# The MLP of a decoder block as two phases of Strassen products, one up phase per chunk and one down phase for all tokens

## The chip, the cores and the metric
The kernel runs on one core of a Trainium2 chip, in one launch. The metric is the device time in microseconds. Before the change it is 2625.07 us, the median of three runs (2624.57 to 2625.38).

## What is computed
One layer of a decoder in float32: 2048 tokens of 1024 channels. A norm and an input projection feed two mixers (a gated linear recurrence and sliding-window attention); their normalised outputs go through an output projection and are added to x. Then comes the MLP, which the change is about, and a last norm:

```
x = x + jnp.einsum('bte,ed->btd', mixed, w_out[l])
hm = rmsnorm(x, norm_mlp_g[l])
up = jnp.einsum('btd,df->btf', hm, w_mlp_up[l])                                          # 1024 -> 4096
x = x + jnp.einsum('btf,fd->btd', jnp.square(jax.nn.relu(up)), w_mlp_down[l])            # 4096 -> 1024
return rmsnorm(x, norm_final_g)
```

## The kernel before
The tokens are worked on in two chunks of T = 1024. Float32 accuracy comes from splitting each operand into two float32r tiles, hi and lo: ACT copies hi, DVE subtracts to get lo (`split_weight`, L141 to 151, for weights that SP's queue loads at L144). Each product takes three matmuls: hi·hi, hi·lo, lo·hi. A matmul has a stationary tile of 128x128 and 512 moving columns.

A chunk passes through `stage1` (norm by `norm_a`, transposes on PE and splits by `norm_b`), the projections with the two mixers, the output projection (loop L673 to 719, its matmul L698, its residual added by DVE at L703), and the MLP (L722 to 788). In the last part of the output projection each of the eight token tiles of 128 tokens is normalised as it is finished, transposed and split, into tiles `hm` that stay in SBUF.

The MLP goes through 32 tiles of 128 hidden channels, two at a time. `up2` makes the two tiles for all 1024 tokens (48 matmuls each); `relu2` takes the relu and the square on ACT and splits on DVE. `down` multiplies the two by their rows of w_down for each token tile (12 matmuls for each tile, L757) and adds the result to the residual `x1[t]` in SBUF at L761. The loop at L781 puts the up of the next two tiles ahead of the down of the present two, so that PE always has matmuls whose operands are ready. Only the last `down` of a chunk normalises and stores, token tile by token tile; in the next to last one of chunk 0, `stage1` of chunk 1 is interleaved. SBUF is held by several pools with slots that follow each other (`U(i, ...)`, slots u0 to u21), and the PSUM banks are the pairs b0/b1, b2, b3 and the double banks mm0, mm1.

The scheduler places an instruction behind what it reads, within the program's order and the slots that are free; each engine then runs its own queue in order.

## Time and profile before
| what | value |
|---|---|
| median of the runs | 2625.07 us (2624.57 to 2625.38) |
| profiled execution: span | 2623.2 us |
| PE | 2577.5 us busy, 13106 instructions |
| DVE | 1474.1 us busy, 2290 instructions |
| ACT | 987.5 us busy, 1713 instructions |
| POOL | 207.4 us busy, 309 instructions |
| DMA | 159.40 MB in 45795 packets |

The span is one execution, from its first to its last recorded instruction. An engine's busy time is the time in which it worked on instructions; beside it stand the intervals in which it waited. The chain of waits follows the instruction that ended last back, step by step, to what released it. The granted clock is TensorE's clock as a share of its full 2.4 GHz.

### The profile page before, as it was taken

How to read it: one execution, taken by the hardware profiler on the slowest of the kernel's cores; microseconds unless marked ns; L12 is line 12 of the kernel's file. 1: busy time of each engine (PE TensorE's matmuls, PEld its weight loads, DVE VectorE, ACT ScalarE, POOL GpSimd, SP SyncE). 2: the span in 40 equal slices, each digit the busy share in tenths (PEclk: the TensorE clock that was granted, in tenths of full speed). 3: DMA queues.
4: the chain of work that ended last, by engine and by line, in shares of the span. 5: the costliest groups of instructions: out<-in, count | busy, mean ns of one | idle time of the engine just before them, and what ended most of it. 6: DMA issues, size and time to landing. Idle time of an engine off the chain costs nothing.

```text
span 2623.2 us, 32045 instructions
## 1 busy us (share of the span) xinstructions
PE 2577.5 (98%) x13106; PEld 2121.0 (81%) x13106; DVE 1474.1 (56%) x2290; ACT 987.5 (38%) x1713; POOL 207.4 (8%) x309
## 2 busy tenths in 40 slices
PE   7999999999999999999999999999999999999998
PEld 6887777788888888888888877778888888888887
DVE  6786658755444444444668866786544444444445
ACT  5666777214111111111446667772231212121212
POOL 1454000000000000000005530010000000000000
PEclk9999999999999999999999999999999999999999
DMA  4111114202111111111331111151021111111101
GB/s 156 41 49 49 44 43 144 92 25 78 44 56 42 57 41 56 41 57 40 112 113 41 50 50 43 43 170 63 17 89 49 49 48 49 48 49 49 48 32 65
DMA packets 45795, 159.40 MB, mean 61 GB/s; under 512 B 5328, under 2 KB 7376, under 8 KB 45648
## 3 DMA queue, kind: packets, MB, share of 16 engines
q1 hardware_dynamic: 39744, 136.12, 15.8%
q0 software_dynamic: 5760, 20.97, 2.2%
q8 instruction: 103, 1.69, 0.3%
q14 instruction: 44, 0.36, 0.0%
q10 hardware_dynamic: 144, 0.26, 0.0%
HBM read 140.56 MB, written 16.78 MB: 60 GB/s over the span
## 4 chain that ended last, share of the span: by engine, by line
PE 84%; DVE 8%; ACT 5%; issue 1%; POOL 1%; DMA 0%; SPq 0%; DVEq 0%; ACTq 0%; POOLq 0%
PE dps L757 26%; PE ops L698 12%; PE pps L194 9%; PE pps L193 9%; PE pps L196 9%; PE sc L350 2%; PE qps L193 2%; PE qps L196 2%; PE qps L194 2%; PE xps L194 1%; PE xps L193 1%; PE xps L196 1%; DVE xc L457 1%; PE av L404 1%; DVE r L630 1%
## 5 line engine op out<-in xcount | busy, mean ns | idle before, releaser
L150 DVE TENSOR_TENSOR wlo<-wraw,whi 128x1024 fp32r<-128x1024 f32 x210 | 260.1, 1243 | 431.4 <-PE pps L194 350.7
L149 ACT ACTIVATE whi<-wraw 128x1024 fp32r<-128x1024 f32 x212 | 223.1, 1056 | 684.5 <-PE dps L757 515.1
L761 DVE TENSOR_TENSOR x<-dps,x 128x512 f32<-128x512 f32 x512 | 332.9, 685 | 249.4 <-PE dps L757 249.1
L194 PE MATMUL pps<-ht,whi 128*128 128x512 f32 x1024 | 399.1, 390 | 0.0
L193 PE MATMUL pps<-ht,whi 128*128 128x512 f32 x1024 | 399.1, 390 | 0.0
L196 PE MATMUL pps<-ht,wlo 128*128 128x512 f32 x1024 | 326.3, 390 | 0.0
L757 PE MATMUL dps<-wlo,fhi 128*128 128x512 f32 x1024 | 317.1, 390 | 0.7 <-DVE wlo L150 0.5
L757 PE MATMUL dps<-whi,fhi 128*128 128x512 f32 x1024 | 316.4, 390 | 0.0
L757 PE MATMUL dps<-whi,flo 128*128 128x512 f32 x1024 | 316.1, 389 | 0.0
L698 PE MATMUL ops<-whi,ht 128*128 128x512 f32 x1024 | 282.5, 394 | 0.0
L728 ACT ACTIVATE s<-pps 128x1024 f32<-128x1024 f32 x56 | 57.5, 1027 | 493.1 <-PE pps L196 493.1
L698 PEld LDWEIGHTS ops<-whi,ht 128*128 128x128 f32 x1024 | 191.5, 188 | 44.0 <-DVE x L703 1.9
L757 PEld LDWEIGHTS dps<-wlo,fhi 128*128 128x128 f32 x1024 | 192.0, 188 | 41.7 <-DVE wlo L150 1.5
L757 PEld LDWEIGHTS dps<-whi,flo 128*128 128x128 f32 x1024 | 192.1, 188 | 40.7
L194 PEld LDWEIGHTS pps<-ht,whi 128*128 128x128 f32 x1024 | 192.3, 188 | 40.4
L196 PEld LDWEIGHTS pps<-ht,wlo 128*128 128x128 f32 x1024 | 192.3, 188 | 40.2
L193 PEld LDWEIGHTS pps<-ht,whi 128*128 128x128 f32 x1024 | 192.3, 188 | 40.1
L757 PEld LDWEIGHTS dps<-whi,fhi 128*128 128x128 f32 x1024 | 191.5, 188 | 39.7 <-ACT whi L149 0.4
L698 PE MATMUL ops<-wlo,ht 128*128 128x512 f32 x512 | 161.5, 395 | 0.0
L364 ACT ACTIVATE st<-sc,mx 128x128 f32<-128x128 f32 x256 | 91.4, 363 | 63.3 <-DVE mx L361 62.8
L698 PEld LDWEIGHTS ops<-wlo,ht 128*128 128x128 f32 x512 | 95.6, 188 | 22.0 <-DVE wlo L150 0.5
L732 DVE CAST fhi<-s 128x1024 fp32r<-128x1024 f32 x64 | 44.2, 690 | 117.2 <-ACT s L729 117.2
(200 smaller groups left out, 3854.5 us busy)
## 6 DMA issues: line engine op xcount, KB each, us to landing
wraw<-in_w_up_dram SPq DMA_DIRECT2D x64, 512.0 KB, 3.4
wraw<-in_w_down_dram SPq DMA_DIRECT2D x64, 512.0 KB, 3.4
wraw<-in_w_in_dram SPq DMA_DIRECT2D x52, 512.0 KB, 3.4
wraw<-in_w_out_dram SPq DMA_DIRECT2D x32, 512.0 KB, 3.5
xt<-in_x_dram SPq DMA_DIRECT2D x16, 512.0 KB, 4.1
ydr<-yt POOLq DMA_DIRECT2D x16, 512.0 KB, 2.9
yre<-ydr SPq DMA_DIRECT2D x16, 512.0 KB, 3.4
x<-in_x_dram POOLq DMA_DIRECT2D x16, 512.0 KB, 4.1
```

What stands on the lines that cost most here:

```text
L149: act.activation(hi, raw, AF.Copy)
L150: (eng or dve).tensor_tensor(lo, raw, f32(hi), op=ALU.subtract)
L193: pe.matmul(ps[m], w[0][:, k * P:(k + 1) * P], ht[m][0][:, k, :], start=(k == 0), stop=False)
L194: pe.matmul(ps[m], w[0][:, k * P:(k + 1) * P], ht[m][1][:, k, :], start=False, stop=False)
L196: pe.matmul(ps[m], w[1][:, k * P:(k + 1) * P], ht[m][0][:, k, :], start=False, stop=(k == KT - 1))
L350: pe.matmul(sc[:, i, :], self.q[:, b * P:(b + 1) * P], keys(self.kv, pt, b), start=(pt == 0), stop=(pt == 1))
L364: ins = act.activation(self.st[:, b, :], cur[:, i, :], AF.Exp, bias=self.mx[:, b:b + 1], accum_out=self.ls[:, b:b + 1])
L698: pe.matmul(ps[m], a_, wk[k][b_][:, hs], start=(k == 0 and a_ is yh and b_ == 0), stop=(k == kn - 1 and a_ is ylo))
L728: act.activation(s, ps, AF.Relu)
L732: dve.tensor_copy(hi, s)
L757: pe.matmul(ps[m], a_, wk[k][b_][:, hs], start=(k == 0 and a == 0 and b_ == 0), stop=(k == 1 and a == 1))
L761: dve.tensor_tensor(xs_, ps[m], xs_, op=ALU.add)
```

## The change
The up and the down product are cut into quarters, and each is made with seven products of quarters in place of eight.

Up: `Up` holds for a chunk the transposed tokens in the form of seven right operands: B11, B21, B22 and T2 are made as the output projection finishes its token tiles (`token_tile`), T4, T3 and T1 by `sums` behind it. A pair `fp` stands for two tiles of hidden channels. `weights(fp)` loads them, POOL makes sums S1, S2, S4 and A12 - A22 as float32, and ACT and DVE split all into hi and lo. `pair(fp)` runs seven products of 12 matmuls, some on top of others in one PSUM bank (S2 and S3 on A11's in pa, S4 on S1's in pr). ACT and DVE bring the results together into c1, c2, and DVE makes from their squares the seven left operands of the down products, which go to DRAM (`actd`, seven stores of 256 KB, each partition in two pieces of 1 KB). The residual x1 goes to DRAM too (`x1d`).

Down: after both chunks, PSUM becomes four tiles of two banks. `Down(g)` loads a group of four tiles of w_down and makes T1, T2, T3 and (in `split`) T4 on POOL; `act_load` brings the left operands of a block of 512 tokens back and splits them. For each g (8) and blk (4) there are seven products of 12 matmuls; after each, DVE adds its PSUM tile of 128x1024 to the residual. The next g's weights are split in block 3, one or two behind each product. `finish` normalises and stores a block in the last g.

In the output projection's last part, transposes are made for two token tiles at a time, here and in stage1 (`flip2`). All SBUF pools become one pool with fixed tags. `stage1` of chunk 1 moves into the last pair of chunk 0. Attention and the recurrence keep their work.

```diff
-    def norm_b(xn, ht, t, ps=None):
+    def norm_b(xns, ht, tp, banks):
...
+        def token_tile(self, t, src, g):
...
+            for q in range(2):
+                o12, o22 = os[q], os[2 + q]
+                t1, x3, y2 = self.braw[q][:, :, ts], self.x3[q][:, :, ts], self.y2[q][:, :, ts]
+                dve.tensor_tensor(t1, o12, t1, op=ALU.subtract)
+                act.activation(x3, o12, AF.Copy)
+                dve.tensor_tensor(y2, o22, t1, op=ALU.subtract)
+                hq = self.h["T2"]
+                act.activation(hq[0][q][:, :, ts], y2, AF.Copy)
+                dve.tensor_tensor(x3, o22, x3, op=ALU.subtract)
+                dve.tensor_tensor(hq[1][q][:, :, ts], y2, f32(hq[0][q][:, :, ts]), op=ALU.subtract)
+                hq = self.h["B22"]
+                split_ps(o22, hq[0][q][:, :, ts], hq[1][q][:, :, ts])
+        def sums(self):
...
+            for q in range(2):
+                dve.tensor_tensor(t4[q], t4[q], self.y2[q], op=ALU.subtract)
+            split("T4", ("u16", "u17", "u18", "u19"), t4)
+            split("T3", ("u6", "u3", "u5", "u4"), self.x3)
+            split("T1", ("u8", "u9", "u2", "u7"), self.braw[:2])
...
+        def weights(self, fp):
...
+            act.activation(a1h, r1, AF.Copy)
+            dve.tensor_tensor(a1l, r1, f32(a1h), op=ALU.subtract)
...
+            pool.tensor_tensor(s12[:, 0], r2[:, lo], r2[:, hi], op=ALU.add)
+            pool.tensor_tensor(s12[:, 1], s12[:, 0], r1[:, lo], op=ALU.subtract)
+            pool.tensor_tensor(r2[:, lo], r1[:, lo], r2[:, lo], op=ALU.subtract)
+            pool.tensor_tensor(r1[:, hi], r1[:, hi], s12[:, 1], op=ALU.subtract)
...
+        def pair(self, fp):
...
+            self.prod(pa, fp, "S3", "T3", False)
+            s3 = small.tile([P, HALF], F32, name="s3", tag="s3", bufs=1)
+            act.activation(s3, pa, AF.Copy)
+            c2 = self.hidden()
+            dve.tensor_tensor(c2[:, lo], pq, s3, op=ALU.add)
+            yield
+            self.prod(pr, fp, "S1", "T1", True)
+            dve.tensor_tensor(c2[:, hi], pr, s3, op=ALU.add)
...
+            self.prod(pr, fp, "S4", "B22", False)
+            dve.tensor_tensor(c1[:, hi], pr, sc[:, 1], op=ALU.add)
...
+            for o, y in enumerate((c1[:, lo], c2[:, hi], a12[:, 1], c2[:, lo], c1[:, hi], a4, a12[:, 0])):
+                nc.sync.dma_start(actd[self.c][g][:, :, o, r * 2 * P:(r + 1) * 2 * P],
+                                  y.rearrange("p (s n) -> p s n", s=2))
...
+    ps_stack.close()
+    ddp = ctx.enter_context(tc.tile_pool(name="ddp", bufs=4, space=PSUM, reuse_waits="tile"))
...
+        def split(self, name):
+            if name == "T4":
+                b21 = self.raw["B21"]
+                pool.tensor_tensor(b21, b21, self.raw["T2"], op=ALU.subtract)
+                self.raw["T4"] = b21
+            self.w[name] = split_to(BW[name], self.raw[name], name)
...
+    PRODS = (("A11", "B11", 0, (0,)), ("A22", "T4", 1, (2,)), ("S2", "T2", 0, (1,)),
+             ("A12", "B21", 2, (0,)), ("S3", "T3", 0, (2,)), ("S4", "B22", 1, (1,)),
+             ("S1", "T1", 0, (3,)))
+    SPLITS = (("B11",), (), ("T2",), ("B21", "T4"), ("T3",), ("B22",), ("T1",))
...
+        pool.tensor_tensor(four[1], four[1], four[2], op=ALU.add)
+        pool.tensor_tensor(four[1], four[1], four[3], op=ALU.subtract)
...
+    def finish(blk):
...
+        dve.tensor_tensor(a12, a12, a22, op=ALU.add)
+        dve.tensor_tensor(a12, a12, a21, op=ALU.subtract)
+        for i in range(2):
+            for h_, (l_, r_) in enumerate(((a11, a12), (a21, a22))):
+                ss = [sumsq(y[:, i, :], "fin") for y in (l_, r_)]
+                act.activation(ss[0], ss[1], AF.Identity, bias=ss[0])
+                rs = rstd_of(ss[0], 1, "fin")
...
+    for g in range(NG):
+        nxt = None
+        for blk in range(NB):
...
+                for d_ in dst:
+                    dve.tensor_tensor(accs[blk][d_], o, accs[blk][d_], op=ALU.add)
+                if last and nxt:
+                    for nm in SPLITS[n]:
+                        nxt.split(nm)
+                if n == 1 and blk == 1 and g + 1 < NG:
+                    nxt = Down(g + 1)
+                if n == 2 and (g + 1 < NG or not last):
+                    gn, bn_ = divmod(g * NB + blk + 1, NB)
+                    nops = act_load(gn, bn_)
```

How it moves instructions, at two places. The first is on PE in the middle of the up work. Before, its rows are the up product of one tile, pps from whi and wlo:

```order
L196 MATMUL pps_6291<-ht_5463,wlo_6288 128x512
L193 MATMUL pps_6291<-ht_5461,whi_6287 128x512
L194 MATMUL pps_6291<-ht_5462,whi_6287 128x512
L193 MATMUL pps_6291<-ht_5463,whi_6287 128x512
L194 MATMUL pps_6291<-ht_5464,whi_6287 128x512
L196 MATMUL pps_6291<-ht_5461,wlo_6288 128x512
L196 MATMUL pps_6291<-ht_5463,wlo_6288 128x512
```

After the change, the last four rows of the next pair's product on pb come between S1's and S4's products on qr; hm_5487 and its like are parts of B21 and B22, s4 is the split of S4:

```order
L385 MATMUL qr_6952<-hm_6001,s12l_6856 128x512
L385 MATMUL pb_7090<-hm_5489,a1h_6985 128x512
L385 MATMUL pb_7090<-hm_5487,a1l_6986 128x512
L385 MATMUL pb_7090<-hm_5487,a1h_6985 128x512
L385 MATMUL pb_7090<-hm_5489,a1h_6985 128x512
L385 MATMUL qr_6952<-hm_5819,s4_6863 128x512 [waits DVE_49]
L385 MATMUL qr_6952<-hm_5821,s4_6863 128x512
```

The matmuls on qr that add S4 now wait for DVE, which no row of the up product did before; the 12 matmuls of S1 end just ahead of the first row shown.

The second place is DVE in the down work. Before, around a turn from one pair of hidden tiles to the next, with wlo the split of a weight and x1 the residual:

```order
L150 TENSOR_TENSOR wlo_8198<-wraw_8195,whi_8197 128x1024 [waits DMAHW6_49,Activation_49]
L761 TENSOR_TENSOR x1_4601<-dps_8055,x1_4601 128x512 [waits PE_49]
L761 TENSOR_TENSOR x1_4601<-dps_8056,x1_4601 128x512 [waits PE_49]
L150 TENSOR_TENSOR wlo_8204<-wraw_8201,whi_8203 128x1024 [waits DMAHW7_49,Activation_49]
L150 TENSOR_TENSOR wlo_8338<-wraw_8335,whi_8337 128x1024 [waits DMAHW0_49,PE_49]
L732 CAST fhi_8129<-s_8126 128x1024 [waits Activation_49]
L733 TENSOR_TENSOR flo_8130<-s_8126,fhi_8129 128x1024 [waits DVE_49]
L150 TENSOR_TENSOR wlo_8400<-wraw_8397,whi_8399 128x1024 [waits DMAHW1_49,PE_49]
L761 TENSOR_TENSOR x1_4587<-dps_8207,x1_4587 128x512 [waits PE_49]
```

After the change, at the end of a g's block 3 and the start of the next g's block 0; T3l, T4l, B22l, T1l are weight splits, al and as1 splits of left operands, acc the residuals:

```order
L949 TENSOR_TENSOR T3l_16763<-braw_16437,T3h_16762 128x1024 [waits Activation_49]
L949 TENSOR_TENSOR T4l_16746<-braw_16439,T4h_16745 128x1024 [waits Activation_49]
L949 TENSOR_TENSOR al_16718<-araw_16715,ah_16717 128x1024 [waits DMAHW5_49,PE_49,Activation_49]
L1061 TENSOR_TENSOR acc_16280<-dd_16672,acc_16280 128x1024 [waits DVE_49]
L992 TENSOR_TENSOR as1_16723<-araw_16721,as1_16723 128x512 [waits DMAHW6_49,Activation_49]
L949 TENSOR_TENSOR B22l_16780<-braw_16441,B22h_16779 128x1024
L1061 TENSOR_TENSOR acc_16284<-dd_16654,acc_16284 128x1024
L949 TENSOR_TENSOR T1l_16797<-t1_16443,T1h_16796 128x1024 [waits Activation_49]
L1061 TENSOR_TENSOR acc_16183<-dd_16800,acc_16183 128x1024 [waits PE_49]
L1061 TENSOR_TENSOR acc_16187<-dd_16814,acc_16187 128x1024 [waits PE_49]
L949 TENSOR_TENSOR al_16844<-araw_16841,ah_16843 128x1024 [waits DMAHW0_49,Activation_49]
L1061 TENSOR_TENSOR acc_16185<-dd_16800,acc_16185 128x1024 [waits PE_49]
```

The accumulations that read dd from PSUM stand in one queue with the seven weight splits of the next g, where before two weight splits and two splits of hidden tiles stood between 16 additions.

## Rows read from the trace of the kernel before
**Rows 1.** The page's busy time, share of the span and instructions of each engine.
```profile
PE 2577.5 (98%) x13106; PEld 2121.0 (81%) x13106; DVE 1474.1 (56%) x2290; ACT 987.5 (38%) x1713; POOL 207.4 (8%) x309
```

**Rows 2.** Busy us of each engine by stretch, with granted clock, DMA share, GB/s.
```profile
0.00:25.00 25.00, 13.37 (x57) 10.69 (x58) 18.96 (x35) 19.16 (x38) 6.79 (x11) 1.00 0.85 322
...
618.00:663.00 45.00, 45.00 (x205) 36.97 (x204) 16.96 (x20) 15.79 (x23) 0.00 (x0) 1.00 0.34 116
663.00:1275.00 612.00, 612.00 (x2700) 506.22 (x2700) 264.91 (x343) 116.92 (x126) 0.00 (x0) 1.00 0.15 48
...
2570.00:2624.00 54.00, 45.39 (x199) 36.75 (x197) 35.24 (x54) 16.42 (x32) 0.00 (x0) 0.96 0.20 78
```

**Rows 3.** The chain of waits, chunk 0's MLP: start us, us, what.
```profile
615.80 1.93 PE tps L184 x16
...
663.66 21.80 PE dps L757 x96
...
707.23 21.80 PE dps L757 x96
```

**Rows 4.** Groups by line and shape: busy us, mean ns, then idle before.
```profile
L761 DVE TENSOR_TENSOR x<-dps,x 128x512 f32<-128x512 f32 x512 | 332.9, 685 | 249.4 <-PE dps L757 249.1
...
L150 DVE TENSOR_TENSOR wlo<-wraw,whi 128x1024 fp32r<-128x1024 f32 x210 | 260.1, 1243 | 431.4 <-PE pps L194 350.7 <-ACT whi L149 51.3 <-PE kps L194 11.5
L149 ACT ACTIVATE whi<-wraw 128x1024 fp32r<-128x1024 f32 x212 | 223.1, 1056 | 684.5 <-PE dps L757 515.1 <-PE ops L698 141.5 <-DMA wraw<-in_w_out_dram 22.0
...
L733 DVE TENSOR_TENSOR flo<-s,fhi 128x1024 fp32r<-128x1024 f32 x64 | 78.2, 1221 | 1.2
...
L703 DVE SCALAR_TENSOR_TENSOR x<-ops,rs_lr,x 128x512 f32<-128x512 f32 x64 | 45.2, 746 | 60.2 <-PE ops L698 60.2
...
L174 DVE SCALAR_TENSOR_TENSOR xn<-x,rs_mlp,g 128x1024 f32<-128x1024 f32 x16 | 20.5, 1284 | 0.5
...
L457 DVE SCALAR_TENSOR_TENSOR xc<-xps,vec,xc 128x1022 f32<-128x1022 f32 x16 | 20.4, 1276 | 0.0
...
L431 DVE TENSOR_TENSOR acca<-acca,yq 128x512 f32<-128x512 f32 x28 | 18.6, 701 | 7.0 <-ACT yq L428 7.0
...
L639 POOL TENSOR_TENSOR accq<-accq,r 128x1024 f32<-128x1024 f32 x2 | 4.7, 2362 | 3.3 <-ACT r L638 3.3
```

**Rows 5.** The timeline, chunk 1's last down: start us, us, engine, line.
```profile
2604.43 0.62 PE L757 MATMUL dps<-whi,flo 128*128 128x512 f32 x2
...
2604.86 0.69 DVE L761 TENSOR_TENSOR x<-dps,x 128x512 f32<-128x512 f32 x1 [0.18 <-PE dps L757]
```

**Rows 6.** The timeline of POOL beside chunk 0's output projection.
```profile
457.76 2.36 POOL L639 TENSOR_TENSOR accq<-accq,r 128x1024 f32<-128x1024 f32 x1 [1.66 <-ACT r L638]
```

**Rows 7.** The timeline of DVE in the same stretch.
```profile
457.82 3.51 DVE L646 SCALAR_TENSOR_TENSOR ht<-yre,vec,ht 128x512 fp32r<-128x512 f32 x2
```

**Rows 8.** The timeline at the end of the kernel.
```profile
2615.54 0.39 PE L757 MATMUL dps<-whi,flo 128*128 128x512 f32 x1
...
2616.20 0.63 ACT L163 ACTIVATE junk<-x 128x512 bf16<-128x512 f32 x1 [0.31 <-DVE x L761]
2616.73 0.19 ACT L163 ACTIVATION_READ_ACCUMULATOR junk<-x 128x1 f32 x1
...
2618.03 0.29 ACT L156 ACTIVATE rs_fin<-ss_fin,epst 128x1 f32<-128x1 f32 x1
2618.36 0.16 DVE L157 RECIPROCAL rs_fin<-rs_fin 128x1 f32<-128x1 f32 x1 [0.35 <-ACT rs_fin L156]
...
2620.00 0.37 ACTq L771 DMA_DIRECT2D out_dram<-x  x1
```

**Rows 9.** What PE waited for: us in total, times, longest us.
```profile
PE tps L184 <- DVE prevm L127: 7.8, 1, 7.8
```

**Rows 10.** The page's DMA queues: packets, MB, share of 16 engines' time.
```profile
q1 hardware_dynamic: 39744, 136.12, 15.8%
```

More of the change, by code (lines that the diff above doesn't have):

```diff
@@ L166, in new_h, with hk @@
     def new_h():
-        return [[hpool.tile([P, KT, HALF], F32R, name="ht", tag="ht") for _ in range(2)]
-                for _ in range(2)]
+        return [[[H(n, part, kp, "ht") for kp in range(KT // 2)] for part in range(2)]
+                for n in range(2)]
+    def hk(parts, k):
+        return parts[k // 2][:, k % 2, :]
     def norm_a(src, xn, g, nm):
@@ L238, in steps @@
                 g = load(t, g)
[L239 to L242 removed]
+            for tp in range(NT // 2):
+                for t in (2 * tp + 2, 2 * tp + 3):
+                    if t < NT:
+                        load(t, g)
+                if c == 0 and tp % 2:
+                    ps = pair(0, "tps") + pair(1, "tps")
+                else:
+                    ps = mm_halves("tps", 0) + (mm_halves("tps", 1) if c == 0 else pair(0, "tps"))
+                norm_b([xs.pop(2 * tp), xs.pop(2 * tp + 1)], ht, tp, ps)
@@ L779, in hybrid_block_kernel @@
-        steps = None
-        prev = up2(0)
-        for f0 in range(0, NF, 2):
-            cur = prev
-            if f0 + 2 < NF:
-                prev = up2(f0 + 2)
-            if f0 + 4 == NF and c + 1 < NCH:
-                hn, steps = stage1(c + 1)
-            down(f0, cur, steps, f0 + 2 == NF)
-            steps = None
+                        nc.sync.dma_start(x1d[c][t * P:(t + 1) * P, :], x1[t])
+                        if t == 2:
+                            up.weights(0)
+                        up.token_tile(t, x1[t], g2)
@@ new lines, in hybrid_block_kernel @@
+    for g in range(NG):
+        nxt = None
+        for blk in range(NB):
+            ps = {}
+            last = blk + 1 == NB
+            for n, (an, bn, bi, dst) in enumerate(PRODS):
+                first = bi not in ps
+                if first:
+                    ps[bi] = ddp.tile([P, 2, HALF], F32, name="dd", tag="dd")
+                o = ps[bi]
+                ah, al = ops[an]
+                bh, bl = dn.w[bn]
+                for i in range(2):
+                    for r in range(2):
+                        t0 = r * 2 * P + i * P
+                        for k, (a_, b_) in enumerate(((ah, bh), (ah, bl), (al, bh))):
+                            pe.matmul(o[:, i, :], a_[:, t0:t0 + P], b_[:, r, :],
+                                      start=first and r == 0 and k == 0, stop=r == 1 and k == 2,
+                                      skip_group_check=True)
+                for d_ in dst:
[8 more added lines that the diff above has]
+                    nops = act_load(gn, bn_)
+            ops = nops
+            if g + 1 == NG:
+                finish(blk)
+        dn = nxt
```

369 lines of the change are left out of this document (258 added, 111 removed).

## The prediction
> **What bounds the kernel now.** I read the page's busy shares first: PE is busy for 2577.5 us, 98% of the span of 2623.2, and no other engine passes 56% [rows 1]. Then the stretches [rows 2]: from 663 to 1275 us, the middle of chunk 0's MLP, PE is busy 612.00 of 612.00 us, DVE 264.91, POOL not at all, DMA at 0.15 of its capacity. Nothing but matmuls sets the time there, and the hand-over from the output projection to the MLP (618 to 663) is just as full. The chain of waits gives the price of one matmul: a group of 96 on dps takes 21.80 us, and groups start 43.57 us apart (663.66, 707.23) with 96 up and 96 down matmuls in between [rows 3], so 43.57/192 = 0.2269 us each. The sum below is made against the profiled execution (span 2623.2); the median of the three runs, 2625.1, lies 1.9 above it, and I add that at the end.
>
> **What goes.** Before, a chunk's MLP has 1536 up and 1536 down matmuls of 128x512, 6144 in all. Seven products of 12 make an up pair or a down block, 84; there are 32 of each, 5376. So 768 matmuls go, at 0.2269: **−174.3 us**. This holds only where PE stays full, so the rest is a list of places where it no longer does.
>
> **Up phase.** A pair is 84 × 0.2269 = 19.06 us of PE. Per pair DVE has three splits of 1024 (1.24 each), one of 512, four PSUM adds of 0.69 and four sums of 0.70 [rows 4]: 10.0 us. ACT is near that. POOL has four sums of 512 elements; POOL's 1024 takes 2.36 [rows 4], so half of it, about 1.2 each. All fit under 19. The one tight hand-over is S1 to S4: both go into bank pr, and DVE must read S1 (L418) before S4 is added on top of it. Four matmuls of the next pair lie in between (the order rows ahead). In the trace a matmul that started at 2604.43 let DVE start at 2604.86 [rows 5]; 0.43 + 0.69 + 0.04 = 1.16 us against 5 × 0.2269 = 1.13. That costs 0.03 us a pair; I take **+2** for all 32, from 0 to 30 (0.9 a pair, if nothing covered it).
>
> **Output projection to up, twice.** Each of the last four token tiles now asks DVE for two residuals (0.75), a norm (0.16 + 1.28) and half of ten 512-element operations (0.69): 6.4 us, where PE has 24 matmuls, 5.45. After the last matmul DVE still owes: residual, norm and transposes until about 6.3, then ten operations of 0.69, two sums of 1.22, six splits of 1.24, c1 and a1l, 18.7 more. That is 25.0, with the backlog of four tiles 28.8. PE owns 16 transposes (1.93 for 16 [rows 3]) and 66 matmuls before it needs a1l, 16.9 us. So 11.9, with some waits in the tiles before 13 each: **+26** (8 to 18 each). This was free before (45.00 of 45.00).
>
> **Up to chunk 1's projections.** stage1(1) moves into one pair, and some of its tiles take the place of B22, which the pair's last product reads; norm splits and transposes of a quarter of the chunk follow it. At 1.06 + 1.24 a split: **+8** (3 to 15).
>
> **Up to down.** POOL's T2 and T4 sums (2.36 each) start after the last pair's c1 sum frees a slot (0.43 + 0.69), ACT's split adds 1.06: T4 is ready at 6.9 us, while PE has one product of 2.7 us without it. That is 4.2; the last S1-S4 hop, now bare, 1.2; the third accumulation behind two more POOL sums, 3.5; block 1's splits queued behind the seventh accumulation, 3. **+12** (6 to 22).
>
> **Down.** DVE's accumulation of 128x1024 from PSUM is not in the trace. Nearest lies L457, 128x1022 from PSUM at 1.276; below it L733, 1024 from SBUF at 1.221, above it two adds of 0.685, 1.37 [rows 4]; I take 1.25, nearest to L457, which also has one input in PSUM. Blocks 0 to 2 of a g: 7 × 1.25 + 3 × 1.24 + 0.70 = 13.2 us against 19.06, free. Block 3 carries the seven weight splits of the next g as well, 8.7 more: 21.9 against 19.06, and in DVE's order (ahead) the seventh accumulation stands behind six of them. The four PSUM tiles let PE run ahead, but the next block's second tile waits for the seventh accumulation's place in the queue. There is a second cost. When POOL ran a 1024 sum from 457.76 to 460.12 [rows 6], two DVE operations with both inputs in SBUF took 3.51 us [rows 7] where 512 elements take 0.75 each (L703's form, [rows 4]): one of them stood until POOL was done. The T4 sum runs in block 3, and T3's split would stand so. Laid out by hand, the seventh accumulation ends at about 25.2 us of a block in which PE wants its tile at 21.8: 3.4 us, seven times, **+24** (1 to 6 each: 7 to 42).
>
> The Trainium skill, page "SBUF — State Buffer", section "Who interferes with whom", says the same of the two engines: a VectorE operation with two SBUF inputs and a GpSimd operation that reads SBUF take one shared port pair in turn, whole instruction by whole instruction, and one that reads PSUM does not. This speaks against a change that adds some 170 POOL sums; the trace agrees (3.51 us in place of 1.5). By that rule the sum is as it stands; without it the +24 would be about +9, since 2.2 of each 3.4 us is that wait.
>
> **Last g, tail, start.** finish() puts 9.1 us of DVE into each of the last blocks, 22.3 against 19.06 where two follow each other: **+6** (2 to 10). Before, the last output's DMA is issued at 2620.00, 4.5 us after the last matmul's start at 2615.54 [rows 8]. After, it needs 0.43, the accumulation 1.25, two sums of 1.22, then on ACT seven sums of squares (0.63 + 0.19), eight of 0.29 and three DMA issues of 0.37, together 9.2, then 0.16 + 2 × 0.75 on DVE: 15.0. **+10** (8 to 13). Transposing by twos at the start: **+1** (−1 to 4).
>
> **Sum.** −174 + 2 + 26 + 8 + 12 + 24 + 6 + 10 + 1 = −85, a span of 2538, and with the 1.9 us **2540**. All costs at their low ends are 41 (time 2492), at their high ends 172 (time 2623).
>
> **Rivals.**
> (a) *The hand-overs hide.* PE's order shows it can take later products early, and the trace's waits of PE in all of the kernel before are small, 7.8 us the longest [rows 9]. If only the tail, a part of the start of up and 1 us per g are paid, 35 us: 2625 − 174 + 35 = 2486. Against it: DVE's sums for T3, T4 and T1 are plain work with nothing beside it. 12%.
> (b) *DVE sets the pace of down.* If the accumulation costs 1.37 and the weight splits shift further, 6 us at each of seven turns and 2 us more in each of the other 24 blocks: +18 + 48, 2606. For it: the queue is in order and block 3 is over-full; against it: blocks 0 to 2 have 6 us of room. 8%.
> (c) *Slower than before: the stores of up.* Each pair writes seven arrays of 256 KB in pieces of 1 KB, 1792 packets, beside 1 MB of loads. Queue q1 used 15.8% of 16 engines for 39744 packets [rows 10], 0.167 us for one of 3.4 KB. If a 1 KB packet takes as long, a pair needs (1792 + 256) × 0.167/16 = 21.4 us of DMA, more than PE's 19.06; if it takes time by its bytes, 8.8. The buffers a12, a4 and hidden are rewritten each pair, so a DMA bound becomes PE's. It decides against the change where a pair takes 85/32 = 2.7 us more than 19.06, from 0.17 us a packet with nothing lost to gaps. At 24 us a pair, 0.19 us a packet, the time is 2540 + 32 × 4.9 = 2697. Against it: the first 25 us moved 322 GB/s [rows 2], a pair wants 151. 6%.
> (d) *The clock falls after the new gaps.* The granted clock is 1.00 in all stretches with PE full, and also in the first 25 us, where PE worked 13.37 of 25.00 and once waited 7.8; only the last stretch has 0.96 [rows 2, 9]. If the 62 us of new gaps in the forecast were each followed by as long at 1.2 GHz instead of 2.4, 31 us are lost: 2571. 4%. The Trainium skill, page "TensorE: Matmul & The Clock Gate", Part 1, has the clock fall after idling; the first 25 us here do not show it.
> That it does not drop the matmuls is no rival: the order of PE's rows has 84 to a pair and a block.
>
> **How the numbers follow.** The forecast (costs of 41 to 172 us, most likely 60 to 130) has 70%, (a) 12, (b) 8, (c) 6, (d) 4. The range starts at (a)'s 2486, which lies just below the forecast's low end; above it leaves out (c), the half of (b) that passes 2600 and the forecast's last 23 us, together some 15%: **2486 to 2600**. A measurement of this kernel tells apart about 0.2%, 5 us. Faster: all but (c)'s upper half, the forecast's extreme end and a reserve for a stall I have not seen: 0.90; same 0.03; slower 0.07.
>
> **What would show it.** In the profile after: 84 matmuls per 19.1 us in up and in blocks 0 to 2 of down, PE full there; gaps of PE of some 12 us before up's T products, twice; gaps near 3 us at seven turns from block 3 to block 0, ended by DVE's L1061; T3's split near 3.5 us while POOL runs L973; the last matmul some 18 us ahead of the span's end. Wrong if up pairs take over 20 us (S1-S4 or the stores), if the turns have no gap or one in every block, or if matmuls run at 0.44 us after a gap.

## The result and the profile after

The changed kernel takes **2559.45 us** (median of four runs, 2556.74 to 2562.31) against 2624.97 for the kernel before on the same chip: ratio 0.975, 95% interval [0.9736, 0.9764]. The forecast was 2540 in a range of 2486 to 2600. The profiled execution took 2559.54 us, its span is 2557.8: 65.4 less than before's 2623.2, where the sum said 85.

The page of the kernel after: busy times, then the DMA queue of [rows 10].

```profile
PE 2436.4 (95%) x12338; PEld 1983.8 (78%) x12338; DVE 1764.7 (69%) x2377; ACT 1237.1 (48%) x2066; POOL 500.5 (20%) x469
...
q1 hardware_dynamic: 127984, 256.47, 29.7%
```

Against [rows 1], PE has 13106 − 12338 = 768 matmuls fewer, as forecast, but its share of the span fell from 98 to 95%. DVE gained 291 us and POOL 293.

Stretches of the kernel after, in the form of [rows 2]: the middle of an up phase, the down phase behind its first block, and the hand-over between them.

```profile
700.00:900.00 200.00, 200.00 (x867) 160.71 (x866) 110.40 (x125) 99.29 (x116) 62.16 (x43) 1.00 0.43 147
1970.00:2470.00 500.00, 493.59 (x2169) 405.86 (x2168) 394.56 (x333) 147.31 (x153) 64.90 (x25) 1.00 0.38 120
1860.00:1965.00 105.00, 84.45 (x330) 66.18 (x329) 69.58 (x58) 32.50 (x37) 41.85 (x16) 0.90 0.68 230
```

The up phase is full. The down phase lacks 6.4 us in 500. The 105 us around the hand-over lack 20.6, at a mean clock of 0.90. What PE waited for there (us in total, times, longest us):

```profile
PE dd L1057 <- ACT T4h L948: 6.9, 1, 6.9
PE qr L385 <- DVE hid L415: 6.0, 1, 6.0
PE dd L1057 <- DVE acc L1061: 4.4, 3, 3.1
...
```

The 6.9 of the row on T4h only looks like the forecast's "T4 is ready at 6.9 us": the wait forecast there was 4.2, behind one product of PE. In the trace T4's first matmul starts at 1912.67, 10.3 us after the last up matmul (1902.38). The row on L415 is one the forecast did not have: in the last pair of up, S1 must wait until DVE has read A22's half of the same tile.

**Where the time went.** PE's stretches between the starts of the same matmuls in both traces (us):

| stretch | before | after | lost |
|---|---|---|---|
| first matmul to first v transposes | 47.98 | 52.98 | 5.0 |
| to the output projection, both chunks | 747.62 | 747.95 | 0.3 |
| output projection, chunk 0; chunk 1 | 185.83; 185.83 | 192.46; 189.18 | 6.6; 3.4 |
| its end to chunk 1's v transposes | 738.04 | 375.05 | 29.1 over its matmuls |
| chunk 1's last output projection to the last matmul | 702.4 | 974.6 | 54.4 over its matmuls |
| last matmul's start to the end | 7.63 | 18.11 | 10.5 |

The two rows "over its matmuls" leave out what the moved and dropped matmuls take at 0.2269 us: 1728 fewer in the first (392.1), 960 more in the second (217.8). Together 109 us are lost, against 89 in the forecast: −174.3 + 109 = −65.3.

**The clock.** After the change, the granted clock falls to one half, 1.2 GHz in place of 2.4, in nine stretches ahead of the last, each within or behind waits of PE; the records of the kernel before have a fall in the last stretch alone [rows 2]. Two of them with their columns as in [rows 2], and the sums over all nine:

```profile
585.50:592.30 6.80, 5.07 (x13) 4.09 (x14) 4.44 (x5) 1.44 (x3) 0.59 (x1) 0.50 0.19 77
640.00:647.00 7.00, 6.45 (x15) 4.20 (x14) 7.00 (x8) 7.00 (x9) 4.26 (x3) 0.51 0.16 63
...
sum 54.70, PE 43.15 PEld 32.68 DVE 41.04 ACT 28.68 POOL 14.87; mean PE 4.79 PEld 3.63 DVE 4.56 ACT 3.19 POOL 1.65
```

The price, from PE's timeline inside the sixth stretch and just behind the seventh (start us, us, operation): matmuls start 0.43 apart (1893.38, 1893.81), afterwards 0.23 (1903.60, 1903.83).

```profile
1893.38 0.63 PE L385 MATMUL qr<-hm,s12h 128*128 128x512 f32 x1
1893.81 0.63 PE L385 MATMUL qr<-hm,s12l 128*128 128x512 f32 x1
...
1903.60 0.39 PE L1057 MATMUL dd<-B11h,ah 128*128 128x512 f32 x1
1903.83 0.40 PE L1057 MATMUL dd<-B11l,ah 128*128 128x512 f32 x1
```

Some 80 matmuls of 512 columns start in the nine stretches; at 0.2 us each about 16 us are lost there, an estimate from these rows (PE's 43 busy us, halved, bound it at 21.6). It is a price, not a measured cost: where other waits would take its place the clock cost less, and in experiment 6 they did. The costs exceed the forecast by 20 us; how much of that is the clock is not shown.

The 1.00 that [rows 2] gives for the first 25 us of the kernel before is not a measured clock. Its trace has no record of the clock ahead of 22.0 us, and the view counts such time as full. PE's timeline of that kernel shows the lower level there: 128x128 transposes start 0.21 us apart at 13 us, and 0.11 apart at 23 us.

```profile
13.02 1.97 PE L184 MATMUL tps<-ident,xt 128*128 128x128 f32 x8 [0.75 <-DVE ht L188]
...
23.32 0.60 PE L184 MATMUL tps<-ident,xt 128*128 128x128 f32 x4
```

So the kernel before ran at half clock too, from its first matmuls, behind a wait of 7.8 us, to about 22 us.

**DVE beside POOL.** DVE's timeline at the hand-over, then POOL's, in the kernel after:

```profile
1883.04 1.22 DVE L949 TENSOR_TENSOR B11l<-braw,B11h 128x1024 fp32r<-128x1024 f32 x1
1884.17 3.40 DVE L949 TENSOR_TENSOR al<-araw,ah 128x1024 fp32r<-128x1024 f32 x1
1887.50 3.35 DVE L949 TENSOR_TENSOR B22l<-braw,B22h 128x1024 fp32r<-128x1024 f32 x1
1890.78 0.68 DVE L415 TENSOR_TENSOR hid<-qr,s 128x512 f32<-128x512 f32 x1
...
1906.51 2.82 DVE L428 TENSOR_TENSOR a<-hid 128x512 f32<-128x512 f32 x1
...
1942.86 2.34 DVE L1061 TENSOR_TENSOR acc<-dd,acc 128x1024 f32<-128x1024 f32 x2
```

```profile
1883.62 2.87 POOL L965 TENSOR_TENSOR t<-braw 128x1024 f32<-128x1024 f32 x1 [21.54 <-DMA act<-hid]
1886.57 3.20 POOL L967 TENSOR_TENSOR braw<-braw 128x1024 f32<-128x1024 f32 x1
...
1903.09 2.41 POOL L1015 TENSOR_TENSOR acc<-acc 128x1024 f32<-128x1024 f32 x1
1905.46 3.32 POOL L966 TENSOR_TENSOR t<-braw,t 128x1024 f32<-128x1024 f32 x1
1908.86 2.67 POOL L973 TENSOR_TENSOR braw<-braw,t 128x1024 f32<-128x1024 f32 x1
...
1942.36 2.81 POOL L967 TENSOR_TENSOR braw<-braw 128x1024 f32<-128x1024 f32 x1
```

A split of 1.22 us takes 3.40 when a POOL sum starts during the operation ahead of it: it ends 1.1 us after that sum (1883.62 + 2.87 = 1886.49). A sum of 0.69 takes 2.82. An operation with an input in PSUM does not stand: two accumulations take 2.34 us from 1942.86, inside POOL's L967, and of the 294 additions and subtractions on DVE that read PSUM and start while POOL works, none takes over 1.23. L415 is of that kind, but POOL stood still at 1890.78; it came late because it stands in the queue behind two lengthened splits, and PE waits 6.0 us for it. POOL's own sums take up to 3.32 where an undisturbed one takes 2.37. T4's delay has POOL's queue in it as well: two residual sums (the last is L1015) stand ahead of T2's and T4's sums, L966 and L973, until 1905.5.

### The profile page after: what moved, and what is told of

It reads as the page before. It is cut to its first block, busy times and chain, and to the rows that moved or that the text cites. A ratio compares the mean times of both kernels' runs of the same rounds, so it can differ in the third digit from the quotient of the medians.

```text
span 2557.8 us, 32559 instructions
## 1 busy us (share of the span) xinstructions
PE 2436.4 (95%) x12338; PEld 1983.8 (78%) x12338; DVE 1764.7 (69%) x2377; ACT 1237.1 (48%) x2066; POOL 500.5 (20%) x469
## 3 DMA queue, kind: packets, MB, share of 16 engines
q1 hardware_dynamic: 127984, 256.47, 29.7%
q10 hardware_dynamic: 576, 1.05, 0.1%
## 4 chain that ended last, share of the span: by engine, by line
PE 61%; DVE 15%; issue 12%; ACT 8%; DMA 2%; POOL 2%; POOLq 0%; DVEq 0%; SPq 0%; ACTq 0%
PE ops L916 10%; PE qr L385 10%; PE dd L1057 9%; PE pa L385 9%; PE pb L385 3%; PE sc L568 2%; PE qps L226 2%; PE qps L223 2%; PE qps L224 2%; DVE xc L675 2%; DVE acc L1061 1%; PE xps L224 1%; PE xps L223 1%; PE xps L226 1%; PE av L622 1%
## 5 line engine op out<-in xcount | busy, mean ns | idle before, releaser
L1061 DVE TENSOR_TENSOR acc<-dd,acc 128x1024 f32<-128x1024 f32 x224 | 272.4, 1221 | 130.0 <-PE dd L1057 122.2
L948 ACT ACTIVATE ah<-araw 128x1024 fp32r<-128x1024 f32 x96 | 101.9, 1062 | 327.6 <-PE dd L1057 306.4
L166 ACT ACTIVATE whi<-wraw 128x1024 fp32r<-128x1024 f32 x84 | 88.5, 1055 | 119.6 <-PE ops L916 87.0
L167 DVE TENSOR_TENSOR wlo<-wraw,whi 128x1024 fp32r<-128x1024 f32 x82 | 104.5, 1279 | 38.7 <-PE kps L224 12.0
L949 DVE TENSOR_TENSOR al<-araw,ah 128x1024 fp32r<-128x1024 f32 x96 | 129.4, 1351 | 0.5 <-ACT ah L948 0.5
L223 PE MATMUL qps<-ht,whi 128*128 128x512 f32 x256 | 108.3, 423 | 0.0
L224 PE MATMUL qps<-ht,whi 128*128 128x512 f32 x256 | 101.9, 398 | 0.0
L223 PE MATMUL xps<-ht,whi 128*128 128x512 f32 x256 | 101.5, 396 | 0.0
L226 PE MATMUL qps<-ht,wlo 128*128 128x512 f32 x256 | 101.1, 395 | 0.0
L224 PE MATMUL xps<-ht,whi 128*128 128x512 f32 x256 | 100.9, 394 | 0.0
L223 PE MATMUL gpps<-ht,whi 128*128 128x512 f32 x256 | 100.8, 394 | 0.0
L385 PE MATMUL qr<-hm,s 128*128 128x512 f32 x384 | 98.6, 406 | 1.8 <-DVE hid L418 1.8
L224 PE MATMUL gpps<-ht,whi 128*128 128x512 f32 x256 | 100.1, 391 | 0.0
L973 POOL TENSOR_TENSOR braw<-braw,t 128x1024 f32<-128x1024 f32 x8 | 19.5, 2432 | 396.9 <-issue 396.8
```

The source lines that it names most:

```text
L166: act.activation(hi, raw, AF.Copy)
L167: (eng or dve).tensor_tensor(lo, raw, f32(hi), op=ALU.subtract)
L223: pe.matmul(ps[m], w[0][:, k * P:(k + 1) * P], hk(ht[m][0], k), start=(k == 0), stop=False)
L224: pe.matmul(ps[m], w[0][:, k * P:(k + 1) * P], hk(ht[m][1], k), start=False, stop=False)
L226: pe.matmul(ps[m], w[1][:, k * P:(k + 1) * P], hk(ht[m][0], k), start=False, stop=(k == KT - 1))
L385: pe.matmul(ps, w[a_][:, ks], hk(h[b_], k), start=first and k == 0 and i == 0, stop=k == KT // 2 - 1 and i == 2, skip_group_check=True)
```

## The experiments

Beside each experiment stand runs of the kernel before, and its ratio is to those.

**1. All of the change's sums on DVE instead of POOL.** 168 sums move: four per pair, four per group of down, eight for the blocks' first residuals.

```diff
-    pool = nc.gpsimd
+    pool = nc.vector
```

> All MLP sums that POOL makes (four of 512 per up pair, four of 1024 per down group, eight for the residuals) move to DVE, nothing else. Theory L (POOL's sums are the price of the hand-overs: DVE operations with two SBUF inputs stand while POOL works, 3.40 and 3.35 us in place of 1.22 around 1885 us, and the norm's square root queues on ACT behind a split that waits for POOL): the 30 us lost between 1870 and 1960 us fall to about 15, the 3.8 us wait at 583 us goes, time 2535 to 2545. Theory Q (the hand-overs are the amount of DVE's own work in its queue, so more work there makes them longer): 16 sums of 1.22 us join the queue at the last hand-over and 0.7 x 4 each up pair, time 2565 to 2575. Both: the seven turns in down stay near 1.1 us, since T3's split loses 1.35 us of standing and T4's sum costs 1.22.

Measured: 2523.52 us (2522.05 to 2523.76), ratio 0.9612 [0.9598, 0.9627], **36 us less** than the change, although DVE has more to do. That is theory L's direction, beyond its 2535 to 2545; and no wait is left at the seven turns, where both theories kept 1.1 us. DVE's timeline there at the same hand-over, and PE's waits in the 105 us around it:

```profile
1874.24 0.69 DVE L415 TENSOR_TENSOR hid<-qr,s 128x512 f32<-128x512 f32 x1
1874.84 1.22 DVE L949 TENSOR_TENSOR B22l<-braw,B22h 128x1024 fp32r<-128x1024 f32 x1
```

```profile
PE dd L1057 <- ACT T4h L948: 4.3, 1, 4.3
PE dd L1057 <- DVE acc L1061: 2.6, 2, 1.6
PE qr L385 <- DVE hid L415: 2.4, 1, 2.4
...
```

All splits are back at 1.22 and the waits, small ones included, fall from 20.6 to 10.1 us. By stretches the gain is 5.0 and 1.7 in the output projections, 2.3 and 10.3 in the ups, 16.5 in down. The half-clock stretches shrink as well, from nine to five (37.5 us in place of 54.7).

**2. One product twice.** The fourth product of every group and block of down is computed twice, and the second result overwrites the first; DVE adds it once. That is 32 × 12 = 384 matmuls more.

```diff
+                for rep_ in range(2 if n == 3 else 1):
+                    for i in range(2):
...
```

> Each down block makes its fourth product (A12 with B21) twice, the first thrown away: 12 x 32 = 384 more matmuls, no more work elsewhere. If PE bounds down: + 384 x 0.2269 = + 87.1 us less at most 7.5 us of turns that the longer block may hide, so 2639 to 2647. If DVE or the transfers bound down: under + 40, below 2600.

Measured: 2643.68 us (2641.93 to 2646.85), ratio 1.0071 [1.0054, 1.0088]: **+84.2**, where 384 × 0.2269 = 87.1. So PE does bound the down phase, a matmul there costs nearly its full price, and the −174 of the sum is priced rightly.

**3. A11's and A12's weights earlier.** For pair 1 of up they are loaded and split ahead of the sums for T4, T3 and T1 (`weights_a`, a part of `weights`), the rest behind.

```diff
...
+            part = self.weights_a(1)
...
-                if i == 1:
-                    self.weights(1)
...
+            self.sums()
+            self.weights(1, part)
```

> The load and hi/lo split of the second pair's A11, A12 are written ahead of the sums T4, T3, T1, so that PE has 24 matmuls (5.4 us) more before it needs them. Theory Q (PE waits there for DVE's queue, 25 to 29 us of work after the last output projection): each of the two gaps shrinks by about 4 us, and the half-clock stretch at 640 and 1579 us (2.6 us each by the matmuls that start in it) shrinks or goes: 2546 to 2553. Rival (PE waits for T4's and T3's splits themselves, later now by 1.2 us): 2558 to 2562.

Measured: 2560.33 us (2557.0 to 2563.61), ratio 0.9754 [0.9739, 0.9768]: no gain, as the rival had it. DVE works without a pause from 636 to 661 us there, so what is taken ahead of one operation stands behind another: the last split of the stretch ends at 660.7, in the change at 657.3. That agrees with DVE's total as the bound there; it does not show it alone.

**4. T4's product later.** In the first block of down it moves from second to fifth place.

```diff
+    LATE = tuple(PRODS[i] for i in (0, 3, 2, 4, 1, 5, 6))
...
-            for n, (an, bn, bi, dst) in enumerate(PRODS):
+            for n, (an, bn, bi, dst) in enumerate(PRODS if g or blk else LATE):
```

> In the very first down block alone the product that needs no sum of weights, A12 with B21, comes second, and T4's and T2's come after it. Theory C (PE waits 6.9 us for T4 because POOL makes it last): 2.7 us of work moves into that wait: 3 to 6 us less, 2553 to 2557. Rival (the next wait takes over: the residual's sums on POOL at 1920 us hold the accumulations and with them PSUM): under 2 us less.

Measured: 2564.47 us (2560.12 to 2567.0), ratio 0.9768 [0.9753, 0.9782]: no gain, if anything a loss. PE's waits at the hand-over, of this kernel:

```profile
PE dd L1058 <- DVE acc L1062: 7.7, 3, 3.7
PE qr L385 <- DVE hid L415: 6.0, 1, 6.0
PE dd L1058 <- ACT T4h L948: 4.2, 1, 4.2
```

T4h's wait falls from 6.9 to 4.2, the accumulations' rises from 4.4 to 7.7: one wait took the place of the other.

**5. POOL busy beside the kernel of experiment 1.** Eight POOL sums of 512 elements that nobody reads, per group of down; DVE still makes all the real ones. If POOL's share of the memory is the cause, these must cost time; if only the late sums were, they are free.

```diff
+            for k in range(8):
+                z = small.tile([P, HALF], F32, name="s3", tag="s3", bufs=1)
+                nc.gpsimd.tensor_tensor(z, b11[:, k % 2], b22[:, k % 2], op=ALU.add)
```

> The kernel no_pool (2523.5 us) and beside it POOL sums that nobody reads: for each group of down weights eight of 512 elements, about 10 us, as soon as two of its weights have landed. Theory L (what costs is that DVE operations with two SBUF inputs stand still while POOL works): in the hand-over to down, DVE's splits and sums of 1.22 us become 2 to 3.5 us where POOL runs beside them, the sum of its first product comes later, and 3 to 8 us are lost there; in the middle of down, where DVE has room, next to nothing: 2526 to 2532. Rival (what cost was that POOL's results came late; standing beside it is harmless): 2522 to 2525.

Measured: 2531.85 us (2528.74 to 2533.94), ratio 0.9645 [0.9631, 0.9659], **8.3 us more** than experiment 1. POOL's timeline in this kernel, then DVE's:

```profile
1879.53 16.16 POOL L970 TENSOR_TENSOR s<-braw 128x512 f32<-128x512 f32 x8 [479.33 <-DVE hid L418]
```

```profile
1886.71 2.28 DVE L966 TENSOR_TENSOR t<-braw,t 128x1024 f32<-128x1024 f32 x1
1888.92 1.75 DVE L428 TENSOR_TENSOR a<-hid 128x512 f32<-128x512 f32 x1
```

L966 takes 2.28 us instead of 1.22 and L428 1.75 instead of 0.68, beside sums whose result goes nowhere, and PE's wait for T4h at this hand-over grows from 4.3 to 8.8. That is the wait itself, apart from any dependency.

**6. PE kept busy at the starts of up.** 24 matmuls whose result is overwritten, ahead of pair 1 in both chunks (two further times A12's product).

```diff
+            if fp == 1:
+                for _ in range(2):
+                    self.prod(pb, 0, "A12", "B21", True)
```

> The changed kernel with 24 matmuls whose result is thrown away, written where PE waits for DVE at the start of each up phase (just before the second pair's products). Theory K (after the gaps there TensorE runs at half its clock for a while, which costs 2.6 us at each place): the granted clock at 640 and at 1579 us stays 1.00, the 5.4 us of thrown-away work lies in the waits, 2553 to 2558. Rival (the clock's fall comes from elsewhere, or the thrown-away work delays the transposes): the clock still falls, 2559 to 2566.

Measured: 2560.27 us (2557.48 to 2562.01), ratio 0.9753 [0.9739, 0.9768]: no gain. The same stretch as above (640) in this kernel, and the one at chunk 1's start of up:

```profile
640.00:647.00 7.00, 5.53 (x21) 3.17 (x19) 7.00 (x8) 6.80 (x9) 3.42 (x2) 1.00 0.17 68
1579.00:1585.00 6.00, 4.35 (x11) 2.90 (x11) 6.00 (x5) 5.01 (x7) 5.15 (x3) 0.73 0.00 0
```

The half clock at 640 is gone, and at 1579 partly: the clock did as theory K had it, the time as its rival. In each chunk 24 × 0.2269 = 5.4 us of matmuls came on top and cost nothing, so PE had been waiting there anyway, and a clock that falls in such a place costs little.

**7. A shorter tail.** Squares are summed as each quarter is done, and the two halves are normalised together.

```diff
+        for k in (0, 2, 3):
+            squares(k)
...
+        squares(1)
+        for h_, (l_, r_) in ((1, (a21, a22)), (0, (a11, a12))):
```

> Only the last norm of a block is written differently: squares summed per tile as each is final (a11, a21, a22, then a12), four roots in two instructions, the second half's rows scaled first. Forecast's step (the chain of ACT and DVE behind the last matmul, 15.0 us, sets the end): about 10.5 us of it remain, the end comes 13 to 14 us after the last matmul in place of 18.0: 2554 to 2556. Rival (the eight output transfers set the end): 2558 to 2561.

Measured: 2559.24 us (2555.93 to 2561.98), ratio 0.975 [0.9735, 0.9764]. In the profile the tail itself shrank from 18.11 to 15.16 us, but the whole did not move. The time is the rival's; its reason, the output transfers, is not shown. The last matmul starts at 2539.74 in the change and 2544.27 here, the last issue of a store at 2554.56 and 2554.75: 3 us less in the tail and 4.5 more ahead of it, where the four runs of either kernel spread by 6.

**8. No POOL sums, no POOL splits at the start, and the tail of 7.**

```diff
-    pool = nc.gpsimd
+    pool = nc.vector
...
-            wkv = [split_weight(w_in[KT * 3 + i], eng=nc.gpsimd) for i in range(2)]
+            wkv = [split_weight(w_in[KT * 3 + i]) for i in range(2)]
```

> no_pool with the tail's edit, and the two key/value weight splits at the kernel's start on DVE in place of POOL. no_pool was 2523.5; the tail gives 4 to 5; at the start a 128x8 operation of 0.17 us stood 2.26 us beside POOL's split and held the transposes behind it, 1 to 4: 2514 to 2519. Rival (the two splits, 2.4 us more in DVE's queue there, give it back): 2518 to 2521.

Measured: 2522.59 us (2519.23 to 2526.74), ratio 0.9616 [0.96, 0.9632]. It lies above both expectations; beside experiment 1's 2523.52 it is no difference that these runs can tell.

**9. POOL's sums replaced at the hand-over alone** (first group of down and the residuals' quarters), POOL elsewhere.

```diff
+            pool = nc.gpsimd if g else dve
+            self.pool = pool
...
-                pool.tensor_tensor(b21, b21, self.raw["T2"], op=ALU.subtract)
+                self.pool.tensor_tensor(b21, b21, self.raw["T2"], op=ALU.subtract)
...
-        pool.tensor_tensor(four[1], four[1], four[2], op=ALU.add)
-        pool.tensor_tensor(four[1], four[1], four[3], op=ALU.subtract)
+        dve.tensor_tensor(four[1], four[1], four[2], op=ALU.add)
+        dve.tensor_tensor(four[1], four[1], four[3], op=ALU.subtract)
```

> Only the sums at the last hand-over move from POOL to DVE: the first group's four and the residuals' eight. no_pool took 36 us off in all. If the last hand-over holds what POOL's sums cost: down's first blocks lose 14 to 16 us less, nothing else moves, 2543 to 2549. If the loss there is the order of the queues and no_pool's gain lies in up and at the turns: under 6 us, 2554 to 2559.

Measured: 2552.64 us (2547.23 to 2554.79), ratio 0.9722 [0.9708, 0.9737]: 6.8 less than the change, between the two expectations. L415's wait falls from 6.0 to 2.5 and T4h's from 6.9 to 4.4, but the accumulations' rises to 6.1. POOL's timeline there shows what stands beside them:

```profile
1932.50 3.25 POOL L968 TENSOR_TENSOR t<-braw,t 128x1024 f32<-128x1024 f32 x1
```

Free of the first group's sums, POOL makes the next group's from 1929.9 to 1938.5 (one of the three is shown), beside the first blocks of down, where DVE is still behind.

**10. T4's sum on DVE at the seven turns alone**, POOL elsewhere.

```diff
+            self.pool = dve if g else nc.gpsimd
...
-                pool.tensor_tensor(b21, b21, self.raw["T2"], op=ALU.subtract)
+                self.pool.tensor_tensor(b21, b21, self.raw["T2"], op=ALU.subtract)
```

> Only T4's sum of the groups after the first moves from POOL to DVE, seven operations. The forecast had 3.4 us at each of seven turns, measured were 1.08, and no_pool had none, where I had expected 1.1 to stay. If the wait of T3's split beside POOL (2.57 in place of 1.22 us) is all of a turn: no wait at the seven turns, 7 us less, 2551 to 2554. If the turns went because T1's to T3's sums left POOL too: 1 us stays at each, 2558 to 2561.

Measured: 2552.58 us (2550.26 to 2557.07), ratio 0.9727 [0.9713, 0.9742]: 6.9 less. In the change PE's only waits of that kind between 1965 and 2480 us were these, in this kernel there is none:

```profile
PE dd L1057 <- DVE acc L1061: 6.4, 7, 0.9
```

Seven waits of 0.9 us, one in each block 0 behind a turn, and gone with seven POOL sums: the mechanism of the forecast at a quarter of its size.

**11. Gaps put into the kernel before**, to see the clock without the change: 24 copies of a weight tile onto itself on ACT, at four places of chunk 0's MLP.

```diff
+            if c == 0 and f0 in (8, 14, 20, 26):
+                for _ in range(24):
+                    act.activation(wk[1][0], f32(wk[1][0]), AF.Copy)
```

> The kernel before, in which TensorE's clock is 1.00 throughout, with 24 copies of a weight onto itself put in a row on ACT at four places of chunk 0's MLP, so that PE stands there for some 8 to 15 us. Theory K (a wait of PE is followed by a stretch at half clock): the time grows by PE's waits and 2.5 to 3.4 us more at each of the four places, and the granted clock shows four stretches of 0.5. Rival (the clock falls for another reason than waits): the time grows by the waits alone, clock 1.00.

Measured: 2627.16 us (2626.55 to 2627.63), ratio 1.0009 [0.9999, 1.0019]. The experiment failed: no gap arose. From 900 to 1000 us, where one of the bursts lies, PE was busy 99.72 us, at clock 1.00. It says nothing of the clock. It shows that ACT had room there: four bursts of 24 copies of 1.05 us, some 100 us of work, cost 2.5 us (2626.55 to 2627.63 against 2624.06 to 2625.61).

**12. Experiment 8 with the order of 4.** The diffs are those two together.

> best1 with t4_late's order of products in the first down block. There PE waits 4.3 us for T4's split, and the residuals' sums, now on DVE, are done early, so that the wait that took over in t4_late (accumulations behind POOL's sums) is gone: the way from the last up product through the first two blocks gets 2 to 4 us shorter, 2518 to 2521. Rival: DVE's queue (sums, splits) is what PE waits for there, whatever the order: 2521 to 2524.

Measured: 2525.02 us (2524.74 to 2527.17), ratio 0.9622 [0.9608, 0.9636]: above both expectations; the order gains nothing without POOL's sums either. The fastest kernels remain those of experiments 1 and 8, some 2523 us, 1.4% below the change and 3.9% below the kernel before.

## Why the prediction was right, and where its steps were off

The direction, the size and the range held: the costs came to 109 us, inside the stated 41 to 172. The agreement is partly luck, errors that cancel, so each term is set against its measure. The turns and the last g were too large by 21 us together, and the hand-overs, S1 to S4 and the start too small by some 40.

| term | forecast | measured, in part estimated |
|---|---|---|
| 768 matmuls | −174.3 | −174.3, priced |
| S1 to S4, 32 pairs | 2 | about 10.5 |
| output projection to up, both | 26 | about 28 |
| stage1(1), up to chunk 1 | 8 | about 15 |
| up to down | 12 | about 30 |
| seven turns | 24 | about 8 |
| last g | 6 | about 1 |
| tail | 10 | 10.5 |
| start | 1 | 5.0 |

Start and tail are stretches of the table above. The others divide its long stretches by counting matmuls at 0.2269 us, and where one term ends and the next begins can shift 2 to 6 us between neighbours: the hand-over to up comes to 34 when all of 627.02 to 716.64 and 1565.12 to 1656.00 is given to it.

**The signs that were named.** From the second g on, blocks take 19.04 us, a little over 20 in block 0 behind each of the seven turns, where a gap is ended by L1061; and the last matmul starts 18.1 us ahead of the end. So far it is as told. The gaps of some 12 us ahead of up's T products are not there: the waits come in pieces, the longest 2.1 us. And one of the signs of being wrong came true: matmuls 0.43 us apart behind gaps. The sum had no term for the clock. Rival (d) had it, and set against it the first 25 us of the kernel before; against what (d) says of them, they show half clock behind a wait, and so speak for it.

**The matmuls** are right: experiment 2 prices 384 of them at 84.2 us where 87.1 was due.

**Up, S1 to S4: too small.** A pair takes 19.40 us in place of 19.06. PE's timeline in the kernel after, one pair's first S1 to the next one's:

```profile
716.64 0.73 PE L385 MATMUL qr<-hm,s12h 128*128 128x512 f32 x2
...
736.04 0.74 PE L385 MATMUL qr<-hm,s12h 128*128 128x512 f32 x2
```

The step counted one hand-over of 0.03; there are two, since S1 also waits for L415 to read the other half of the same tile. PE's matmuls start late at these two places alone, and together they cost 0.34 a pair, inside the term's 0 to 30. It is not POOL's doing: without its sums a pair still takes 19.38.

**Output projection to up: right in size**, 26 against about 28, **but not by the wait it named.** The step let PE wait for a1l at the end of DVE's debt. In experiment 3 a1l's split starts at 645.45 in place of 654.91 and nothing is gained; PE's waits in the change are mostly for the hm splits (L331, L343). That the debt as a whole sets the time is argued. Something was left out as well: at 583 us the square root of a norm stood in ACT's queue behind a split that waited for POOL's sum, and PE waited 3.8 us for the norm (1.1 in experiment 1, where no split waits for POOL). POOL's timeline, then ACT's:

```profile
581.33 1.29 POOL L363 TENSOR_TENSOR s<-s,wraw 128x512 f32<-128x512 f32 x1
```

```profile
582.66 1.06 ACT L367 ACTIVATE s12h<-s 128x1024 fp32r<-128x1024 f32 x1 [3.16 <-POOL s L363]
583.62 0.28 ACT L173 ACTIVATE rs_mlp<-ss_mlp,epst 128x1 f32<-128x1 f32 x1
```

**Up to chunk 1: inside 3 to 15.** The largest single wait, 5.5 us, is one that the step did not name: PE's for the split of a weight tile of chunk 1's first projection (kps, L223). SP issues that load at 963.73, behind two stores of the last pair and two loads of stage1. No run moved that load; in experiment 1 the wait is 5.5 us as well.

**Up to down: mis-sized, 12 against 30**, above its 6 to 22. This is the step that failed most. It had a wait of 4.2 us for T4 where 6.9 were measured, since two residual sums run on POOL ahead of T2's and T4's. Beyond that it missed two things. The first is the wait of DVE on POOL, which the forecast had applied to the turns and not here, although here POOL has four sums of weights and two of residuals: splits of 3.40 and 3.35 us, L415 behind them, PE's 6.0. Taking those sums away there (experiment 9) removed L415's and T4h's excess, and moved part of it to the accumulations. The second is the clock, at half for four stretches (20.4 us) around this hand-over; what it cost there no run separates.

**The turns: mis-sized, 24 against 8.** Right in mechanism, as experiment 10 shows: seven gaps, ended by L1061, gone without the POOL sum. The place is one step further on: PE waits at T2's product of block 0 for that block's first accumulation, which has the seventh of block 3 and T1's split ahead of it in DVE's queue. The size was wrong in both of its parts. T3's split was expected at 3.5 us and takes 2.57: POOL's sum began 0.92 us before the split did (DVE's timeline, then POOL's, one turn of the kernel after):

```profile
1992.44 1.22 DVE L1061 TENSOR_TENSOR acc<-dd,acc 128x1024 f32<-128x1024 f32 x1
1993.58 2.57 DVE L949 TENSOR_TENSOR T3l<-braw,T3h 128x1024 fp32r<-128x1024 f32 x1
```

```profile
1992.66 2.40 POOL L973 TENSOR_TENSOR braw<-braw,t 128x1024 f32<-128x1024 f32 x1 [47.50 <-issue]
```

And DVE's work was added up by durations, where rows show starts closer together. In experiment 1's turn, operations of 1.22 us start 1.13 to 1.14 apart:

```profile
1971.34 1.22 DVE L1061 TENSOR_TENSOR acc<-dd,acc 128x1024 f32<-128x1024 f32 x1
1972.47 1.22 DVE L949 TENSOR_TENSOR B22l<-braw,B22h 128x1024 fp32r<-128x1024 f32 x1
1973.61 1.22 DVE L1061 TENSOR_TENSOR acc<-dd,acc 128x1024 f32<-128x1024 f32 x1
```

The accumulation itself takes 1.221 us, below the 1.25 assumed. Block 3 has 18 such operations (seven accumulations, three splits, one sum, seven weight splits); at 0.09 each that is 1.6 us. With the 0.94 of T3's split (3.51 less 2.57) it makes 2.5, an estimate that meets the difference between the 3.4 of the forecast and the 0.9 measured.

**The last g and the tail:** 1 against 6, below its 2 to 10, probably for the same overlap; 10.5 against 10.

**The start: 5 against 1**, above its −1 to 4. A DVE operation on 8 columns stood for 2.26 us (the next one of that size, at 25.05, took 0.17) while POOL split a weight; a norm queued behind it, and PE waited 5.4 us. That is at most a small part of the cause: in experiment 8, with these splits on DVE and the operation back at 0.17, PE still waits 4.3 us and 3.3 of the 5.0 are still lost; experiment 5's profile, which keeps POOL's splits there, loses 3.5. The rest stays open. DVE's timeline in the change, then POOL's:

```profile
22.76 2.26 DVE L793 TENSOR_TENSOR aab<-vec,sneg 128x8 f32<-128x8 f32 x1
```

```profile
20.32 4.67 POOL L167 TENSOR_TENSOR wlo<-wraw,whi 128x1024 fp32r<-128x1024 f32 x2 [18.57 <-ACT whi L166]
```

**The rivals.** (a) falls: the waits did not hide, 109 us against 35. (b) falls: the accumulation takes 1.221 us, and blocks without splits have no wait in [1965, 2480]. (c) falls: q1 moved 127984 packets in 29.7% of 16 engines' span, 0.297 × 16 × 2557.8/127984 = 0.095 us each, below the 0.17 from which stores would decide, and PE is full in up at a DMA share of 0.43. (d), given 4%, is partly what happened: the clock fell behind new gaps, for about 16 us by the matmul rows, or less where other waits take its place, against its 31.

The Trainium skill, page "SBUF — State Buffer", section "Who interferes with whom", states that VectorE and GpSimd exclude each other on a shared port pair. The runs agree: 3.40 us for 1.22 beside POOL's sums, 2.34 unchanged for two accumulations that read PSUM, and 8.3 us for sums that nobody reads (experiment 5). The forecast used the rule for the turns alone, where it bore on the hand-over too.

**What stays open.** Why the clock falls in these nine stretches and not in others with similar waits: in experiment 1 PE was busy only 16.12 of the 24 us from 628 to 652, at 1.00. The experiment meant for that (11) made no gap. What the clock cost in all is estimated and not measured. How the 36 us of experiment 1 divide between DVE's shorter operations and the clock was not separated. Experiments 9 and 10, each with one place cleared, give 7 us each of it; experiment 1's stretches put 6.7 on the output projections and 2.3 on chunk 0's up; some 13 are not assigned.

## What to carry to other kernels

When work is moved to POOL to relieve DVE, price the DVE operations that run beside it, not only POOL's time: here 168 sums moved back to the fuller engine were worth 36 us. Apply such a price at every place where it can occur, above all at hand-overs, where the queue behind the lengthened operation holds what PE needs next. Add up a dense queue from start to start, not by durations; and after each new gap of PE, keep the cost of the clock in the range.

## What the runs showed of the hardware

- A DVE operation with both inputs in SBUF beside POOL's work: 128x1024 from 1.22 to 3.40 us, 128x512 from 0.69 to 2.82, 128x8 from 0.17 to 2.26: the wait has little to do with the operation's own size. POOL's sum lengthens too, from 2.37 to 3.32. Operations with an input in PSUM keep their time.
- Back-to-back DVE operations of 1.22 us start 1.13 to 1.14 us apart.
- Nine stretches of granted clock 0.50 behind waits of PE, 54.7 us in all, with matmuls 0.43 us apart in place of 0.23. The kernel before ran at half clock as well behind its first wait of 7.8 us, up to about 22 us: transposes 0.21 apart, then 0.11. Which waits are followed by a fall differs from kernel to kernel. Four runs of the change spread by 5.6 us, four of the kernel before by 0.8.
- 24 ACT copies in a burst, four times, some 100 us of work, cost the kernel before 2.5 us of 2625.
